# One retention normalisation recorded after a gate projection, and a table load recorded inside a contraction

## The chip, the cores and the metric

The kernel runs on one core of one Trainium2 chip. The metric is the device time of one execution in microseconds (us), as the median of several runs. Its engines are named as in the profile: PE (TensorE, matrix products), PEld (its weight loads), DVE (VectorE), ACT (ScalarE), POOL (GpSimd) and SP (SyncE, which issues the transfers). Each has one queue and takes its instructions in the order of that queue, and waits on semaphores where it needs another engine's result.

## The reference

The computation is one hybrid decoder layer on 256 tokens of width 1024, in float32: a SwiGLU block, a mixer, and a second SwiGLU block, each behind an RMS normalisation that a condition vector modulates. Cut to the mixer and to the branch that the change touches:

```python
def retention_branch(q, k, v, g, positions, norm_w):
    ...
    scores = jnp.einsum('bclhd,bcshd->bchls', qc, kc) * decay_mask
    y_intra = jnp.einsum('bchls,bcshe->bclhe', scores, vc)
    ...
    y = (y_intra + y_inter).reshape(bsz, s, h_, dv).astype(v.dtype)
    y = rms_normalize(y).reshape(bsz, s, RET_V_DIM) * norm_w
    return y * jax.nn.silu(g)

def hybrid_mixer(u, ...):
    proj = u @ w_in
    z, xbc, dt_raw, q, k, v, g, gate_ssd_raw, gate_ret_raw = jnp.split(proj, splits, axis=-1)
    y_ssd = ssd_branch(...) @ w_br_ssd
    y_ret = retention_branch(...) @ w_br_ret
    gate_ssd = jax.nn.sigmoid(gate_ssd_raw + gate_b_ssd)
    gate_ret = jax.nn.sigmoid(gate_ret_raw + gate_b_ret)
    return (gate_ssd * y_ssd + gate_ret * y_ret) @ w_out
```

There are 8 retention heads. Each has a score product, a value product of 256 columns, its own RMS normalisation, and a gate silu(g).

## The kernel before, in words

**Products.** Nearly every product with a weight runs as three PE passes: both operands are split into a rounded high part and a low rest, and `mm3` (L143 to L151) adds high·high, low·high and high·low. A weight block of 128x2048 numbers comes by one transfer on SP's queue into one of four staging buffers (`wst`). `half` (L130) then makes two operands of it: ACT rounds 1024 columns (L135, a CAST into `wh`) and DVE subtracts (L136). There are four `wh` buffers, so two weight blocks are in hand at a time. `pair_project` (L293) uses one block: 24 PE passes for each of two `wh` buffers, 48 in all. `split_into` (L139) does the same to an activation tile of 128x512: L140 on ACT, L141 on DVE.

**PSUM.** Two pools of four buffers each: `proj` for the weight products, `misc` for everything else. A `misc` buffer is handed to a new tile only when the last reader of the old one is done.

**The retention steps.** Three steps work on a head `n`, and one on a pair of heads:

- `rs.n` (`ret_scores`): two PE products (L876, L877) into a `misc` buffer, and two DVE products with the decay mask (L879, L880). The DVE rows are the last readers of that buffer.
- `rv.n` (`ret_values`): four PE products (L888, L889 twice) into a `misc` buffer `py`, a square on ACT (L891), a sum on DVE (L892), and the split of that sum (`sqh` on ACT L767, `sql` on DVE L768).
- `rn.n` (`ret_norm`): `rstd` multiplies that split by a matrix of ones (two PE products, L219, into another `misc` buffer), then ACT does Ln and Exp (L181, `rs`), DVE refines the root in four instructions (L224, L225, L226, L227; L225 is the last reader of the mean's buffer), two DVE instructions multiply `py` by it and the norm weight (L902, the last readers of `py`), one multiplies by the gate (L905), and `split_into` makes the operands (L140, L141) that the branch product reads.
- `br.p.q` (`branch`): the product of head pair `p` with one half `q` of `w_br_ret`, 48 passes. It needs `rn` of both heads of the pair.

`g.h.p` (`silu_half`) is one gate projection and a Silu on ACT (L181). `ada` is one piece of the condition product: one transfer, and two DVE instructions over 128x1024 (L193).

**Tables.** Ln and Exp lie in one function table of ACT, Silu in another, Sigmoid in a third. `need` (L572) notes which table is loaded and records a load (L173) when the next step wants another; `table` ties a load behind every lookup of the table before it.

**What sets the order.** `ORDER` (L52) is a string of step names; the steps are recorded in that order. A scheduler then lays out each engine's queue: a step that was recorded earlier goes first, but an instruction whose operands it takes to be late is passed by others. So the queues differ from `ORDER` in detail, and one step moved can reorder the queues for some 200 instructions around it.

**The end of the mixer.** After `ORDER` the two branches are combined, the table for Ln and Exp is loaded (L939), and `contract` (L328) multiplies by `mix_w_out` in four blocks. After each output tile the residual's closing function adds it and squares it; after each block `each` is called, which here records a piece of `ada`. Then `modulated` (L259) normalises, with the Ln and Exp in `rstd`.

## Time and profile before

| What | Value |
|---|---|
| median of 3 runs | 835.44 us (835.42 to 836.02) |
| the profiled execution: own time, span of its instructions | 836.0 us, 833.9 us |
| granted PE clock, mean | 0.998 |
| busy: PE, PEld, DVE, ACT, POOL | 820.4, 795.0, 664.1, 517.2, 10.3 us |
| table loads on ACT | 30, each 1.283 us |
| DMA | 193.13 MB, 232 GB/s on average |

The span runs from the first to the last instruction; the execution's own time is 2.1 us longer. A PE row of the timeline is shown with its modelled end, and rows overlap since the products are pipelined: what counts is the distance from one start to the next. "Idle" in a row is time in which an engine had nothing running, and the name behind it is what ended that.

### The profile page before, as it was taken

The numbers are of one execution on the slowest core, as the hardware profiler recorded it, in microseconds if no ns is written. First come the engines' busy times: TensorE is split into PE (matmuls) and PEld (weight loads), VectorE is DVE, ScalarE is ACT, GpSimd is POOL, SyncE is SP. The second block draws the span as 40 slices with busy tenths as digits, with TensorE's granted clock in tenths as the row PEclk, the third lists the DMA queues.
The fourth block names the chain that finished last, engine by engine and source line by source line (L and its number), as shares of the span: only waits on it lengthen the run. The fifth ranks groups of instructions, "written<-read, shape, count | busy, mean of one in ns | idle before, by whom it ended". The sixth has DMA issues, their size and how long they took to land. (4 is left out here: it accounts for less than half of the span.)

```text
span 833.9 us, 16144 instructions
## 1 busy us (share of the span) xinstructions
PE 820.4 (98%) x6734; PEld 795.0 (95%) x6734; DVE 664.1 (80%) x1002; ACT 517.2 (62%) x743; POOL 10.3 (1%) x21
## 2 busy tenths in 40 slices
PE   7999999999999999999999999999999999999996
PEld 6999999999999989999999999999999999999896
DVE  5999899977989987787898768977979985455463
ACT  6665454555898787766565569665558655545342
POOL 0000000000200010000000000000000000000000
PEclk9999999999999999999999999999999999999999
DMA  9998889854695564536657754645555685455521
GB/s 365 415 398 328 303 330 389 343 193 153 231 312 185 183 215 180 197 132 240 233 181 293 253 202 152 223 182 197 207 202 194 263 326 204 152 203 177 189 90 50
DMA packets 30586, 193.13 MB, mean 232 GB/s; under 512 B 3489, under 2 KB 4129, under 8 KB 10034
## 3 DMA queue, kind: packets, MB, share of 16 engines
q1 hardware_dynamic: 28656, 186.40, 60.4%
q0 software_dynamic: 1568, 5.28, 2.0%
q8 instruction: 52, 0.85, 0.4%
q10 hardware_dynamic: 290, 0.44, 0.2%
q14 instruction: 20, 0.16, 0.1%
HBM read 191.02 MB, written 1.08 MB: 230 GB/s over the span
## 5 line engine op out<-in xcount | busy, mean ns | idle before, releaser
L136 DVE TENSOR_TENSOR wh<-wst,wh 128x1024 fp32r<-128x1024 f32 (+1 forms) x263 | 317.2, 1210 | 109.1 <-ACT wh L135 108.4
L135 ACT CAST wh<-wst 128x1024 fp32r<-128x1024 f32 (+1 forms) x263 | 272.7, 1039 | 169.1 <-PE proj L151 129.8
L149 PE MATMUL proj<-uh,wh 128*128 128x256 f32 (+1 forms) x1160 | 322.3, 278 | 0.0
L150 PE MATMUL proj<-ul,wh 128*128 128x256 f32 (+1 forms) x1160 | 321.8, 277 | 0.1
L151 PE MATMUL proj<-uh,wh 128*128 128x256 f32 (+1 forms) x1160 | 321.3, 277 | 0.0
L150 PEld LDWEIGHTS proj<-ul,wh 128*128 128x128 f32 x1160 | 217.8, 188 | 1.1 <-DVE ul L428 0.3
L151 PEld LDWEIGHTS proj<-uh,wh 128*128 128x128 f32 x1160 | 217.8, 188 | 0.5 <-DVE wh L406 0.2
L149 PEld LDWEIGHTS proj<-uh,wh 128*128 128x128 f32 x1160 | 217.8, 188 | 0.3 <-ACT wh L135 0.2
L149 PE MATMUL proj<-s,wh 128*128 128x256 f32 x312 | 86.9, 280 | 0.3 <-ACT s L140 0.3
L150 PE MATMUL proj<-s,wh 128*128 128x256 f32 x312 | 86.3, 278 | 0.0
L151 PE MATMUL proj<-s,wh 128*128 128x256 f32 x312 | 86.2, 277 | 0.0
L149 PEld LDWEIGHTS proj<-s,wh 128*128 128x128 f32 x312 | 58.4, 188 | 0.7 <-ACT s L140 0.5
L150 PEld LDWEIGHTS proj<-s,wh 128*128 128x128 f32 x312 | 58.5, 188 | 0.3 <-issue 0.2
L151 PEld LDWEIGHTS proj<-s,wh 128*128 128x128 f32 x312 | 58.6, 188 | 0.0
L193 DVE SCALAR_TENSOR_TENSOR ada<-ada,cb 128x1024 f32<-128x1024 f32 x48 | 57.5, 1219 | 0.0
L145 PE MATMUL proj<-uh,wh 128*128 128x256 f32 x152 | 42.0, 276 | 0.0
L146 PE MATMUL proj<-uh,wh 128*128 128x256 f32 x152 | 42.0, 276 | 0.0
L147 PE MATMUL proj<-ul,wh 128*128 128x256 f32 x152 | 42.0, 276 | 0.0
L149 PE MATMUL proj<-ah,wh 128*128 128x256 f32 x152 | 42.0, 276 | 0.0
L150 PE MATMUL proj<-al,wh 128*128 128x256 f32 x152 | 42.0, 276 | 0.0
L151 PE MATMUL proj<-ah,wh 128*128 128x256 f32 x152 | 42.0, 276 | 0.0
L181 ACT ACTIVATE s<-proj 128x512 f32<-128x512 f32 x33 | 19.7, 597 | 33.0 <-PE proj L151 32.9
(271 smaller groups left out, 1399.6 us busy)
## 6 DMA issues: line engine op xcount, KB each, us to landing
wst<-in_mix_w_in_dram SPq DMA_DIRECT2D x52, 1024.0 KB, 4.9
wst<-in_ffn_w_in_dram SPq DMA_DIRECT2D x43, 1024.0 KB, 5.8
wst<-in_ffn_w_out_dram SPq DMA_DIRECT2D x17, 1024.0 KB, 5.2
ada<-in_ada_w_dram SPq DMA_DIRECT2D x16, 1024.0 KB, 9.0
wst<-in_ada_w_dram SPq DMA_DIRECT2D x12, 1024.0 KB, 4.9
ada<-in_ada_w_dram SPq DMA_DIRECT2D x16, 512.0 KB, 12.6
wst<-in_w_br_ssd_dram SPq DMA_DIRECT2D x8, 1024.0 KB, 5.7
wst<-in_w_br_ret_dram SPq DMA_DIRECT2D x8, 1024.0 KB, 4.9
```

Source lines behind the costliest of these rows:

```text
L135: act.copy(hi, v)
L136: dve.tensor_tensor(lo, v, hi.bitcast(F32), ALU.subtract)
L145: pe.matmul(o, l[1], r[0], start=False, stop=False, skip_group_check=skip)
L146: pe.matmul(o, l[0], r[0], start=False, stop=False, skip_group_check=skip)
L147: pe.matmul(o, l[0], r[1], start=False, stop=False, skip_group_check=skip)
L149: pe.matmul(o, l[0], r[0], start=first, stop=False, skip_group_check=skip)
L150: pe.matmul(o, l[0], r[1], start=False, stop=False, skip_group_check=skip)
L151: pe.matmul(o, l[1], r[0], start=False, stop=last, skip_group_check=skip)
L181: phase["uses"].append(act.activation(*args, **kw).ins)
L193: dve.scalar_tensor_tensor(st[:, i, :], st[:, i, :], 1.0, cb, ALU.mult, ALU.mult, accum_out=raw[:, j, f0 + i:f0 + i + 1])
```

## The change

Two edits. In `ORDER`, `rn.0 g.1.0` becomes `g.1.0 rn.0`: the normalisation of the first head is recorded after the first gate projection of the second pair. And the load of the table for Ln and Exp is recorded by the function that `contract` calls after each block, the first time it is called, and no longer ahead of `contract`.

```diff
-    "rv.0 rs.1 rv.1 rn.0 g.1.0 ada rs.2 rn.1 rs.3 rv.2 g.1.1 rv.3 br.0.0 rn.2 rn.3 br.0.1 rs.4 g.2.0 "
+    "rv.0 rs.1 rv.1 g.1.0 rn.0 ada rs.2 rn.1 rs.3 rv.2 g.1.1 rv.3 br.0.0 rn.2 rn.3 br.0.1 rs.4 g.2.0 "
...
         while ada_todo[0][0] == 7:
             ada_next()
-        table("natural_log_exp_and_others")
+        later = ["natural_log_exp_and_others"]
+
+        def each():
+            if later:
+                table(later.pop())
+            ada_next(6)
         am = scale_col(V_N3, 7)
...
         contract("mix_w_out", 8, lambda kt: at(mh[kt // 4], al, kt % 4),
-                 residual(5, 1.0, am, ha, u, 6), lambda: ada_next(6))
+                 residual(5, 1.0, am, ha, u, 6), each)
```

What this does to the queues is shown at three places.

**First place: ACT, right after the Silu of the last projection of the first pair, `g.0.1` (`proj_5800`).** `wh_6018` and `wh_6045` before, `wh_6016` and `wh_6043` now, are the weights of `g.1.1`; `misc_5856` and `misc_5874` are the values of heads 0 and 1; `misc_5887` is the mean of head 0; `proj_5889` is the projection `g.1.0`.

```order
 L181 ACTIVATE s_5733<-proj_5800 128x512
-L173 ACT_TABLE_LOAD
+L135 CAST wh_6016<-wst_6013 128x1024
 L891 ACTIVATE rsq_5861<-misc_5856 128x512
-L135 CAST wh_6018<-wst_6015 128x1024
+L135 CAST wh_6043<-wst_6013 128x1024
 L767 ACTIVATE sqh_5864<-rsq_5861 128x256
-L135 CAST wh_6045<-wst_6015 128x1024
 L891 ACTIVATE rsq_5879<-misc_5874 128x512
-L181 ACTIVATE rs_5890<-misc_5887,epsc 128x256
-L181 ACTIVATE rs_5890<-rs_5890 128x256
-L173 ACT_TABLE_LOAD
```

A load and its return are gone here, the weights of `g.1.1` are rounded earlier, and the Ln and Exp of head 0 stand behind the Silu of `g.1.0`. The program has 28 table loads instead of 30. On DVE the subtraction for `wh_6016` and the sum of head 0 (L892) stand ahead of the mask rows L879 and L880 of head 1 (`m_5871`), which were first before:

```order
+L136 TENSOR_TENSOR wh_5917<-wst_5887,wh_5917 128x1024
+L136 TENSOR_TENSOR wh_6016<-wst_6013,wh_6016 128x1024
+L892 TENSOR_TENSOR rsq_5861<-rsq_5861 128x256
 L879 TENSOR_TENSOR m_5871<-misc_5868,xe_5724 128x256
 L880 TENSOR_TENSOR m_5871<-misc_5868,xe_5724 128x128
-L892 TENSOR_TENSOR rsq_5861<-rsq_5861 128x256
```

**Second place: PE between the projection `g.1.1` and the first branch product.** Before, the mean of head 1 (`misc_5979`) and the scores of heads 2 and 3 (`misc_5972`, `misc_5996`) stand ahead of the 48 passes of `g.1.1` (`proj_6017`):

```order
L876 MATMUL misc_5972<-s_4902,s_4970 128x256
L877 MATMUL misc_5972<-s_4902,s_4970 128x128
L219 MATMUL misc_5979<-sqh_5882,onesr 128x256 [waits DVE_49,Activation_49]
L219 MATMUL misc_5979<-sql_5883,onesr 128x256 [waits DVE_49]
L876 MATMUL misc_5996<-s_4902,s_4970 128x256 [waits DVE_49,PE_49]
L877 MATMUL misc_5996<-s_4902,s_4970 128x128
L149 MATMUL proj_6017<-uh_146,wh_6018 128x256
```

Now the mean of head 0 and the scores of head 2 stand ahead of `g.1.1`, and behind its 48 passes follow the mean of head 1 (`misc_5977`), the scores of head 3 (`misc_5994`), the values of head 2 (`misc_6000`) and the first passes of the branch product, whose operand `s_5961`, `s_5962` is the split of heads 0 and 1:

```order
L219 MATMUL misc_5977<-sqh_5882,onesr 128x256 [waits DVE_49,Activation_49]
L219 MATMUL misc_5977<-sql_5883,onesr 128x256
L876 MATMUL misc_5994<-s_4902,s_4970 128x256 [waits DVE_49,PE_49]
L877 MATMUL misc_5994<-s_4902,s_4970 128x128
L888 MATMUL misc_6000<-m_5974,s_3668 128x256 [waits DVE_49]
L889 MATMUL misc_6000<-m_5974,s_3668 128x128
L149 MATMUL proj_6090<-s_5961,wh_6087 128x256 [waits Activation_49]
L149 MATMUL proj_6119<-s_5961,wh_6116 128x256
L149 MATMUL proj_6187<-s_5961,wh_6184 128x256 [waits PE_49]
L149 MATMUL proj_6216<-s_5961,wh_6213 128x256 [waits PE_49,Activation_49]
L150 MATMUL proj_6090<-s_5962,wh_6087 128x256 [waits DVE_49]
```

(L888 and L889 come twice here; the second two are left out.) By the semaphore values, the first of these waits for DVE's L225 of head 0, which frees the mean's buffer, and L876 waits for the second L902 of head 0, which frees `py` of head 0. The first four passes of the branch product go to four different `proj` tiles.

**Third place: DVE, the root of head 1 and what follows it.** Before:

```order
L224 TENSOR_TENSOR rt_5983<-rs_5982 128x256
L225 SCALAR_TENSOR_TENSOR rt_5983<-misc_5979,rt_5983 128x256
L226 TENSOR_SCALAR rt_5983<-rt_5983 128x256
L227 TENSOR_TENSOR rs_5982<-rs_5982,rt_5983 128x256
L768 SCALAR_TENSOR_TENSOR sql_6011<-rsq_6007,sqh_6010 128x256
L902 SCALAR_TENSOR_TENSOR m_5990<-misc_5874,col,rs_5982 128x256 x2
L879 TENSOR_TENSOR m_5999<-misc_5996,st_5970 128x256
```

Now a weight subtraction, the split of head 0 (L141), the sum of head 2 (L892) and both instructions of an `ada` piece (L193) stand between the steps of that root, and L879, L905 and L880 behind them:

```order
L224 TENSOR_TENSOR rt_5981<-rs_5980 128x256
L136 TENSOR_TENSOR wh_6213<-wst_6182,wh_6213 128x1024
L141 TENSOR_TENSOR s_5962<-m_5957,s_5961 128x512
L225 SCALAR_TENSOR_TENSOR rt_5981<-misc_5977,rt_5981 128x256
L193 SCALAR_TENSOR_TENSOR wst_6386,raw<-wst_6386,cb 128x1024
L226 TENSOR_SCALAR rt_5981<-rt_5981 128x256
L892 TENSOR_TENSOR rsq_6005<-rsq_6005 128x256
L227 TENSOR_TENSOR rs_5980<-rs_5980,rt_5981 128x256
L193 SCALAR_TENSOR_TENSOR wst_6386,raw<-wst_6386,cb 128x1024
L902 SCALAR_TENSOR_TENSOR m_5988<-misc_5874,col,rs_5980 128x256 x2
L879 TENSOR_TENSOR m_5997<-misc_5994,st_5969 128x256
```

From the gate projections of the third pair (`g.2.0`, `g.2.1`) on, all queues are again in the order of before, up to the end. That includes the second edit: in ACT's queue the table load for the last normalisation stands where it stood, between the last Sigmoid of the gate (L181) and the CAST of the second half of the first `mix_w_out` block.

## The prediction

> **What bounds the kernel now.** I read the page's busy shares first, then the busy time by stretch around the moved steps and around the last normalisation of the mixer, then PE's own waits, then the timeline of each engine.

> ```profile
> PE 820.4 (98%) x6734; PEld 795.0 (95%) x6734; DVE 664.1 (80%) x1002; ACT 517.2 (62%) x743; POOL 10.3 (1%) x21
> ...
> 480.00:495.00 15.00, 15.00 (x132) 14.95 (x132) 10.99 (x15) 7.80 (x11) 0.00 (x0) 1.00 0.76 267
> 495.00:510.00 15.00, 14.52 (x112) 13.77 (x112) 11.40 (x19) 14.22 (x18) 0.00 (x0) 1.00 0.42 154
> 620.00:640.00 20.00, 19.70 (x172) 19.51 (x171) 18.22 (x32) 15.90 (x31) 0.00 (x0) 1.00 0.45 158
> ...
> PE misc L219 <- ACT sqh L767: 0.5, 1, 0.5
> PE misc L219 <- ACT sq L248: 0.8, 1, 0.8
> ```

> The columns of a stretch are its length, the busy time of PE, PEld, DVE, ACT and POOL, PE's clock, the DMA share and GB/s. PE is never idle from 480 to 495 us and issues 132 passes there, so a pass takes 15.00/132 = 0.1136 us. From 495 to 510 ACT is the one that is full, 14.22 of 15 us, and PE loses 0.48 us to `sqh`. So time is lost or won only where PE waits; whatever else moves is free. PE's order and its waits at the first place:

> ```profile
> 498.57 0.59 PE L888 MATMUL misc<-m,s 128*128 128x256 f32 x2
> 499.88 0.60 PE L876 MATMUL misc<-s,s 128*128 128x256 f32 x2
> 500.45 0.36 PE L149 MATMUL proj<-uh,wh 128*128 128x256 f32 x1
> 501.00 0.28 PE L150 MATMUL proj<-ul,wh 128*128 128x256 f32 x1
> 501.26 0.70 PE L888 MATMUL misc<-m,s 128*128 128x256 f32 x2
> 502.45 0.38 PE L889 MATMUL misc<-m,s 128*128 128x128 f32 x2
> 503.32 0.39 PE L219 MATMUL misc<-sqh,onesr 128*128 128x256 f32 x1 [0.48 <-ACT sqh L767]
> ...
> 511.00 0.28 PE L150 MATMUL proj<-ul,wh 128*128 128x256 f32 x1
> 511.26 0.70 PE L888 MATMUL misc<-m,s 128*128 128x256 f32 x2
> ```

> A head's values take 499.88 - 498.57 = 1.31 us on PE, a head's scores 500.45 - 499.88 = 0.57 us. PE is late three times: L888 at 501.26 where 501.11 was free (0.15), L219 at 503.32 where 501.26 + 1.31 = 502.57 was free (0.75), L888 at 511.26 where 511.11 was free (0.15). That is 1.05 us, and it is all that the first edit can win here.

> **Prices.** ACT and DVE from their timeline and from the groups between 495 and 530 us (count, then busy time and mean ns of one):

> ```profile
> 499.52 0.59 ACT L181 ACTIVATE s<-proj 128x512 f32<-128x512 f32 x1
> 500.13 1.28 ACT L173 ACT_TABLE_LOAD   x1
> 501.42 0.60 ACT L891 ACTIVATE rsq<-misc 128x512 f32<-128x512 f32 x1
> 501.92 1.04 ACT L135 CAST wh<-wst 128x1024 fp32r<-128x1024 f32 x1
> ...
> 617.77 1.28 ACT L173 ACT_TABLE_LOAD   x1
> ...
> L135 ACT CAST wh<-wst 128x1024 fp32r<-128x1024 f32 x10 | 10.4, 1044 | 0.2 <-PE proj L151 0.2
> L173 ACT ACT_TABLE_LOAD x8 | 10.3, 1283 | 0.1
> L181 ACT ACTIVATE rs<-misc,epsc 128x256 f32<-128x256 f32 x4 | 1.9, 474 | 0.3 <-PE misc L219 0.3
> L767 ACT ACTIVATE sqh<-rsq 128x256 fp32r<-128x256 f32 x4 | 1.7, 418 | 0.2 <-DVE rsq L892 0.2
> L181 ACT ACTIVATE rs<-rs 128x256 f32<-128x256 f32 x4 | 1.7, 418 | 0.0
> L140 ACT CAST s<-m 128x512 fp32r<-128x512 f32 x2 | 1.2, 620 | 0.8 <-DVE m L905 0.8
> ```

> ```profile
> 499.64 1.23 DVE L136 TENSOR_TENSOR wh<-wst,wh 128x1024 fp32r<-128x1024 f32 x1 [0.95 <-ACT wh L135]
> 500.79 0.42 DVE L879 TENSOR_TENSOR m<-misc,xe 128x256 f32<-128x256 f32 x1
> ...
> L902 DVE SCALAR_TENSOR_TENSOR m<-misc,col,rs 128x256 f32<-128x256 f32 x6 | 2.6, 477 | 0.0
> L193 DVE SCALAR_TENSOR_TENSOR wst<-wst,cb 128x1024 f32<-128x1024 f32 x2 | 2.4, 1220 | 0.0
> L905 DVE TENSOR_TENSOR m<-m,s 128x512 f32<-128x512 f32 x3 | 2.1, 685 | 0.0
> L892 DVE TENSOR_TENSOR rsq<-rsq 128x256 f32<-128x256 f32 x4 | 1.7, 424 | 1.8 <-ACT rsq L891 1.8
> L225 DVE SCALAR_TENSOR_TENSOR rt<-misc,rt 128x256 f32<-128x256 f32 x4 | 1.7, 422 | 0.1
> L224 DVE TENSOR_TENSOR rt<-rs 128x256 f32<-128x256 f32 x4 | 1.7, 422 | 0.0
> L141 DVE TENSOR_TENSOR s<-m,s 128x512 fp32r<-128x512 f32 x2 | 1.4, 688 | 0.4 <-ACT s L140 0.4
> L227 DVE TENSOR_TENSOR rs<-rs,rt 128x256 f32<-128x256 f32 x3 | 1.3, 424 | 0.1
> L226 DVE TENSOR_SCALAR rt<-rt 128x256 f32<-128x256 f32 x3 | 0.9, 293 | 0.1
> L879 DVE TENSOR_TENSOR m<-misc,st 128x256 f32<-128x256 f32 x2 | 0.8, 416 | 0.0
> L880 DVE TENSOR_TENSOR m<-misc,st 128x128 f32<-128x128 f32 x2 | 0.6, 282 | 0.0
> ```

> An instruction that waits for nothing starts 0.1 us before the last one ends (501.42 + 0.60 against 501.92); a table load starts behind its end. From one engine to another I count 0.05 us (L879 ends at 501.21, L888 starts at 501.26).

> **Part one, what it removes.** Two table loads, 2 x 1.283 us of ACT, and the wait of 0.75 us for `sqh`. The trace shows nothing beside the load itself: 0.1 us of idle time ahead of eight of them, and the next instruction 0.01 us behind. [...]

> **What it moves, walked through in the new order.** All times are those of the old trace up to the Silu at 499.52, and reckoned from there.

> First, the mask of head 1. The CAST of `wh_6016` now follows the Silu directly, 500.02 to 501.06; DVE subtracts 501.11 to 502.33, sums head 0 from 502.25, and comes to L879 at 502.60, which ends at 503.0 where it ended at 501.21. PE has 15 passes ahead of the values of head 1, not five, and is there at 501.11 + 10 x 0.1136 = 502.25. It waits to 503.05: 0.8 us. So the first two old waits, 0.9 us together, come back as one of about their size.

> Second, the bank waits. PE goes on: values 1.31, 33 passes 3.75, two passes for the mean of head 0 (0.23), scores of head 2 (0.57), 48 passes of `g.1.1` (5.45), and stands at 514.35 before the mean of head 1. Meanwhile head 0 is normalised: `g.1.0` ends at 508.3, then Silu, `sqh` of head 1 and the table load run to 510.55, Ln to 511.0, a CAST to 512.0, Exp to 512.3. DVE does a weight subtraction (512.05 to 513.27), L224, and another subtraction whose CAST waits until PE has freed its buffer (513.5 to 514.75); then L225 ends at 515.1, L227 at 515.85, the second L902 at 516.8, L879 at 517.1, L905 at 517.7, L880 at 517.9. PE's next three steps wait for three of these: the mean of head 1 for L225 (515.15, 0.8 us), after 0.23 the scores of head 3 for L902 (516.85, 1.45), after 0.57 the values of head 2 for L880 (517.95, 0.55). In the old order 48 passes of `g.1.1` lay between the mean of head 1 and the branch product; now they are spent before.

> Third, the branch product. The values end at 519.25; the split's high part is ready (Ln and Exp of head 1 to 516.5, load to 517.85, CAST to 518.45), four passes take PE to 519.7, and L141 stands behind a weight subtraction, 519.3 to 520.0: 0.35. Twenty more passes end at 522.3. Now PE needs the mask L879 of head 3 for the next values, and DVE has ahead of it L225, L193, L226, L892, L227, L193 and twice L902: from 519.95 at 0.08 us less than their rows each, with 0.05 where one needs the last one, that is 524.25 for its start and 524.7 for its end: 2.45. L889 then waits for L880, behind L905, to 525.55: 0.25. Then the rest of these values, 0.9 us (1.31 less the first L888), and two passes, to 526.7, and the low part of head 1's split (CAST from 525.35, L141 to 526.7), with which PE goes on at 526.75: 0.05.

> The sum is 0.8 + 0.8 + 1.45 + 0.55 + 0.35 + 2.45 + 0.25 + 0.05 = 6.7 us of waits, for 1.05 us before: 5.65. One wait more is likely and not walked through, the low part of head 3's sum (L768), which now stands behind a weight subtraction: between nothing and 0.3 us, taken as 0.15. That makes 5.8 us. From `g.2.0` on the queues are as before, and PE is full again, so nothing gives it back.

> **Part two costs and gains nothing.** The load at 617.77 stands between the same neighbours in ACT's queue. PE's wait of 0.8 us for the last square (L248) and the normalisation behind it stay.

> **Bounds.** An ada piece is in this chain: its transfer is issued when the subtraction that ends at 513.27 frees its staging buffer. If it were 1 us late, the third wait would grow by that; if each of six more changes between float32 products and passes costs what L149 at 500.45 has over its neighbours (0.36 for 0.28 us), 0.5 us more. The other way, each of the eight waits ends a chain of five to ten instructions, and 0.3 us of error in each is 2.4 us: 3.4 to 7.3 us in all.

> Against the profiled execution: span 833.9 + 5.8 = 839.7 us, own time 836.0 + 5.8 = 841.8 us. That execution is 0.6 us above the median of the runs shown, so the median is expected at 835.44 + 5.8 = 841.2 us; its own range is 838.8 to 842.7.

> **Rivals.**

> (a) Nothing net. DVE is far enough ahead that L225, L902 and L880 are done when PE comes, and the old waits only change place: 835.4 us. For it: DVE was 80% busy, and ACT gains 2.6 us of room. Against: L225 sits behind a subtraction whose CAST needs the first half of `g.1.1` done, which no earlier start of ACT can mend.

> (b) Faster. Both parts do what they are named for: the three waits go (1.05 us), and the wait at the last normalisation (0.8 us), because the load is out of its way: 833.6 us. For it: ACT was full for 15 us at the first place. Against: the load at 617.77 keeps its neighbours, and the three waits are replaced by the eight above.

> (c) A slower clock. PE waits seven times within 12 us. If the clock halves for some time after that, the 24 passes of the branch product's half that follow cost twice 0.1136 us, 2.7 us more: 843.9 us. The point from which it decides is a wait that holds PE long enough; the trace has granted clock 1.00 in every stretch quoted, with waits up to 0.8 us. [...]

> **How the numbers follow.** Forecast 0.85, (a) 0.06, (b) 0.05, (c) 0.04. What a measurement of this kernel can tell from no change is about 0.2%, 1.7 us. (a) lies within, (b) just outside, the forecast and (c) outside on the slow side: faster 0.05, same 0.06, slower 0.89. The range is widened a little past the forecast's own on both sides, towards a half-hidden second group (the three bank waits gone: 838.4) and (c): 838.2 to 843.8.

> **What would show it.** PE's waits by releaser: L219 and L876 on DVE (L225, L902) near 515 and 517, L888 on DVE near 518 and near 525, L150 on L141 near 520; 28 table loads; the stretch 510 to 527 with PE idle 5 to 6 us; the tail's rows shifted by 5.8 us and else as before. It is wrong if PE is full from 505 to 525, or if the shift at `g.2.0` is not the shift at the end.

## The result, and the profile after

| | median | all executions | against before |
|---|---|---|---|
| before | 835.80 us | 835.42 to 836.02 (6) | |
| the change | 841.24 us | 840.70 to 842.54 (6) | 1.0068, 95% interval 1.0059 to 1.0078 |

The change costs 5.4 us; 841.2 was forecast. In its profiled execution the own time is 840.76 us and the span 838.9, against 836.0 and 833.9. (Of all executions in the sections below one, of 2134.2 us in the run with the ada piece moved and filler, was disturbed and is left out.)

Busy time of the whole kernel, and its PE waits (line waited for: us in total, times, longest):

```profile
PE 822.7 (98%) x6734; PEld 796.8 (95%) x6734; DVE 663.8 (79%) x1002; ACT 514.3 (61%) x741; POOL 10.3 (1%) x21
...
PE misc L888 <- DVE m L879: 1.3, 2, 0.7
PE misc L876 <- DVE m L902: 1.2, 1, 1.2
...
PE misc L219 <- DVE rt L225: 0.5, 1, 0.5
```

The wait for `sqh` (L767) is gone, and ACT is 2.9 us less busy. Three waits on DVE take its place: on masks (L879), on L902 and on L225. The busy time by stretch, in the columns of the prediction's first fence:

```profile
495.00:510.00 15.00, 14.41 (x116) 13.90 (x115) 9.27 (x12) 11.07 (x15) 0.00 (x0) 1.00 0.40 151
510.00:525.00 15.00, 12.40 (x83) 11.36 (x81) 12.89 (x26) 9.79 (x14) 0.00 (x0) 0.89 0.44 144
525.00:540.00 15.00, 14.86 (x122) 14.27 (x121) 10.61 (x21) 10.66 (x16) 0.00 (x0) 1.00 0.37 137
```

From 495 to 510 us ACT went from 14.22 us busy to 11.07, and PE gained nothing from it. From 510 to 525 PE issues 83 passes where it issued 124. It stood idle for 2.60 us, and the clock, 1.00 before, is 0.89. That second figure was not in the forecast. PE's timeline there:

```profile
515.19 0.35 PE L219 MATMUL misc<-sqh,onesr 128*128 128x256 f32 x1 [0.50 <-DVE rt L225]
...
516.89 0.67 PE L876 MATMUL misc<-s,s 128*128 128x256 f32 x2 [1.23 <-DVE m L902]
...
520.01 1.20 PE L149 MATMUL proj<-s,wh 128*128 128x256 f32 x4
521.01 0.41 PE L150 MATMUL proj<-s,wh 128*128 128x256 f32 x1
521.23 0.41 PE L151 MATMUL proj<-s,wh 128*128 128x256 f32 x1
...
522.11 0.28 PE L151 MATMUL proj<-s,wh 128*128 128x256 f32 x1
522.23 0.28 PE L149 MATMUL proj<-s,wh 128*128 128x256 f32 x1
...
523.60 0.28 PE L151 MATMUL proj<-s,wh 128*128 128x256 f32 x1
524.61 0.70 PE L888 MATMUL misc<-m,s 128*128 128x256 f32 x2 [0.73 <-DVE m L879]
```

The bank waits stand where they were forecast (515.15 and 516.85). But the branch product's passes at 521 start 0.22 us apart, those at 522 again 0.12. So PE reaches the values of head 3 at 523.7 and not at 522.3, and waits 0.73 us for a mask that I expected it to await for 2.45. In half-microsecond stretches the clock begins to fall inside 518.00 to 518.50 (mean 0.97, so 0.03 us at half) and is back inside 521.50 to 522.00 (mean 0.62, so 0.38 us at half): half clock from 518.47 to 521.88, 3.41 us.

So there are two questions for the runs. Do the waits come from where the walk had them? And what does the half clock cost, which I had as a rival with a chance of 0.04?

### The profile page after: what moved, and what is told of

Same layout as the page of the kernel before. It is cut to its first block, busy times and chain, and to the rows that moved or that the text cites. A ratio compares the mean times of both kernels' runs of the same rounds, so it can differ in the third digit from the quotient of the medians.

```text
span 838.9 us, 16141 instructions
## 1 busy us (share of the span) xinstructions
PE 822.7 (98%) x6734; PEld 796.8 (95%) x6734; DVE 663.8 (79%) x1002; ACT 514.3 (61%) x741; POOL 10.3 (1%) x21
## 5 line engine op out<-in xcount | busy, mean ns | idle before, releaser
L136 DVE TENSOR_TENSOR wh<-wst,wh 128x1024 fp32r<-128x1024 f32 (+1 forms) x263 | 317.0, 1209 | 115.2 <-ACT wh L135 114.6
L135 ACT CAST wh<-wst 128x1024 fp32r<-128x1024 f32 (+1 forms) x263 | 272.5, 1039 | 168.8 <-PE proj L151 130.1
L149 PE MATMUL proj<-uh,wh 128*128 128x256 f32 (+1 forms) x1160 | 322.6, 278 | 0.0
L151 PE MATMUL proj<-uh,wh 128*128 128x256 f32 (+1 forms) x1160 | 321.3, 277 | 0.0
L150 PE MATMUL proj<-ul,wh 128*128 128x256 f32 (+1 forms) x1160 | 321.3, 277 | 0.0
L150 PEld LDWEIGHTS proj<-ul,wh 128*128 128x128 f32 x1160 | 218.0, 188 | 0.6 <-issue 0.2
L149 PEld LDWEIGHTS proj<-uh,wh 128*128 128x128 f32 x1160 | 218.1, 188 | 0.3 <-ACT wh L135 0.2
L151 PEld LDWEIGHTS proj<-uh,wh 128*128 128x128 f32 x1160 | 217.9, 188 | 0.5 <-DVE wh L406 0.2
L149 PE MATMUL proj<-s,wh 128*128 128x256 f32 x312 | 87.2, 282 | 0.3 <-ACT s L140 0.3
L150 PE MATMUL proj<-s,wh 128*128 128x256 f32 x312 | 86.4, 278 | 0.0
L151 PE MATMUL proj<-s,wh 128*128 128x256 f32 x312 | 86.2, 277 | 0.0
L149 PEld LDWEIGHTS proj<-s,wh 128*128 128x128 f32 x312 | 58.8, 190 | 0.7 <-ACT s L140 0.5
L150 PEld LDWEIGHTS proj<-s,wh 128*128 128x128 f32 x312 | 58.9, 189 | 0.3 <-issue 0.2
L151 PEld LDWEIGHTS proj<-s,wh 128*128 128x128 f32 x312 | 58.8, 189 | 0.0
L193 DVE SCALAR_TENSOR_TENSOR ada<-ada,cb 128x1024 f32<-128x1024 f32 x48 | 57.5, 1218 | 0.0
L149 PE MATMUL proj<-ah,wh 128*128 128x256 f32 x152 | 42.0, 276 | 0.0
L150 PE MATMUL proj<-al,wh 128*128 128x256 f32 x152 | 42.0, 276 | 0.0
L151 PE MATMUL proj<-ah,wh 128*128 128x256 f32 x152 | 42.0, 276 | 0.0
L181 ACT ACTIVATE s<-proj 128x512 f32<-128x512 f32 x33 | 19.7, 597 | 34.3 <-PE proj L151 34.3
## 6 DMA issues: line engine op xcount, KB each, us to landing
ada<-in_ada_w_dram SPq DMA_DIRECT2D x16, 512.0 KB, 12.8
```

Source lines behind the costliest of these rows:

```text
L135: act.copy(hi, v)
L136: dve.tensor_tensor(lo, v, hi.bitcast(F32), ALU.subtract)
L149: pe.matmul(o, l[0], r[0], start=first, stop=False, skip_group_check=skip)
L150: pe.matmul(o, l[0], r[1], start=False, stop=False, skip_group_check=skip)
L151: pe.matmul(o, l[1], r[0], start=False, stop=last, skip_group_check=skip)
L181: phase["uses"].append(act.activation(*args, **kw).ins)
```

## Experiments

Theory: the first edit alone makes the loss, by letting a head's mean and scores queue behind `misc` buffers that are freed late, and by the DVE chain behind them. The rivals were a share of the second edit, the half clock as part of the price, and a chain that is late whatever buffers there are. The first four kernels, the next three and the last two were each compared with runs of the kernel before that they share (835.69, 835.71 and 835.74 us).

### Each edit alone

The first edit alone:

```diff
-    "rv.0 rs.1 rv.1 rn.0 g.1.0 ada rs.2 rn.1 rs.3 rv.2 g.1.1 rv.3 br.0.0 rn.2 rn.3 br.0.1 rs.4 g.2.0 "
+    "rv.0 rs.1 rv.1 g.1.0 rn.0 ada rs.2 rn.1 rs.3 rv.2 g.1.1 rv.3 br.0.0 rn.2 rn.3 br.0.1 rs.4 g.2.0 "
```

> This kernel has the first edit alone: the gate projection ahead of head 0's normalisation in the written order; the table load stands ahead of the output contraction as before. Theory (all of the loss comes from the first edit, through PE's waits): 841.2 us, 5.4 us above the kernel before, with the same waits of PE between 510 and 525 us as in the changed kernel, 28 table loads and an end of the profile like the changed kernel's. Rival (the second edit has a share, for good or ill): a time more than 0.8 us away from 841.2 us.

Measured: median 842.49 us (840.69, 842.36, 842.62, 843.41), ratio 1.0078, interval 1.0064 to 1.0092. The whole loss is there. The median is 1.3 us above the changed kernel's, which by the letter of the expectation speaks for the rival. But the fastest executions agree, 840.69 and 840.70, and both kernels have executions near 840.7 and near 842.5. Its profiled execution is one of the longer ones (842.62), and shows why:

```profile
502.13 0.28 PE L147 MATMUL proj<-ul,wh 128*128 128x256 f32 x1
502.99 0.70 PE L888 MATMUL misc<-m,s 128*128 128x256 f32 x2 [0.59 <-DVE m L879]
...
514.44 0.28 PE L151 MATMUL proj<-uh,wh 128*128 128x256 f32 x1
515.22 0.36 PE L219 MATMUL misc<-sqh,onesr 128*128 128x256 f32 x1 [0.50 <-DVE rt L225]
515.41 0.28 PE L219 MATMUL misc<-sql,onesr 128*128 128x256 f32 x1
516.91 0.67 PE L876 MATMUL misc<-s,s 128*128 128x256 f32 x2 [1.23 <-DVE m L902]
...
517.95 0.70 PE L888 MATMUL misc<-m,s 128*128 128x256 f32 x2
...
519.28 0.72 PE L149 MATMUL proj<-s,wh 128*128 128x256 f32 x4
520.02 0.38 PE L150 MATMUL proj<-s,wh 128*128 128x256 f32 x1
...
522.36 0.28 PE L151 MATMUL proj<-s,wh 128*128 128x256 f32 x1
524.63 0.70 PE L888 MATMUL misc<-m,s 128*128 128x256 f32 x2 [2.00 <-DVE m L879]
524.98 0.46 PE L219 MATMUL misc<-sqh,onesr 128*128 128x256 f32 x1
525.43 0.49 PE L889 MATMUL misc<-m,s 128*128 128x128 f32 x2
```

The branch product runs at full clock here (520.02 to 522.36), the wait for the mask is 2.00 us long, and L888 starts at 524.63, as in the changed kernel's 524.61. The half clock comes 7.7 us later, from 526.14 to 529.55, on passes that nothing hides: 3.41 us at half clock are 1.7 us of work lost, and this execution is 1.86 us longer than the changed kernel's profiled one. So the time is about 840.7 us when the half clock falls ahead of a wait, and about 842.5 when it falls behind it. That this also tells the changed kernel's own executions apart is inferred: of them only that of 840.76 us has a trace. The 843.41 us is more than this accounts for.

The second edit alone:

```diff
-        table("natural_log_exp_and_others")
+        later = ["natural_log_exp_and_others"]
+
+        def each():
+            if later:
+                table(later.pop())
+            ada_next(6)
...
-                 residual(5, 1.0, am, ha, u, 6), lambda: ada_next(6))
+                 residual(5, 1.0, am, ha, u, 6), each)
```

> This kernel has the second edit alone: the order of before, and the table load written behind the first part of the output contraction. Theory: the load keeps its neighbours in ACT's queue, PE's wait of 0.8 us for the last square (L248) stays, and the time is that of the kernel before within 0.3 us, 835.7 us. Rival: the load leaves the path of the last normalisation and PE's wait of 0.8 us goes, 834.9 us.

Measured: 835.62 us, ratio 0.9999, interval 0.9991 to 1.0008: nothing. ACT's timeline of this kernel:

```profile
616.46 0.84 ACT L181 ACTIVATE s<-proj,col 128x256 f32<-128x256 f32 x2 [1.62 <-PE proj L151]
617.32 1.28 ACT L173 ACT_TABLE_LOAD   x1
618.61 1.05 ACT L135 CAST wh<-wst 128x1024 fp32r<-128x1024 f32 x1
...
622.52 1.05 ACT L135 CAST wh<-wst 128x1024 fp32r<-128x1024 f32 x1 [2.34 <-issue]
```

The load has its old neighbours. Nor does ACT run short of time behind it: ACT is idle for 2.34 us before the second CAST behind the load, and PE's wait for the last square is 0.8 us as before.

### The DVE chain ahead of head 3's mask

Of head 3's wait I had said that two L193 of an ada piece stand in the chain. This takes them out:

```diff
-    "rs.5 g.2.1 rv.4 ada rv.5 br.1.0 rn.4 rn.5 g.3.0 ada rs.6 br.1.1 rs.7 g.3.1 rv.6 rv.7 br.2.0 "
+    "rs.5 g.2.1 rv.4 rv.5 br.1.0 rn.4 rn.5 g.3.0 ada ada rs.6 br.1.1 rs.7 g.3.1 rv.6 rv.7 br.2.0 "
```

> The changed kernel with one piece of the adaptive vectors' work (ada), two L193 of 1.22 us on DVE, moved later by seven steps, out of the queue ahead of head 1's second L902 and the mask L879 of head 3. Theory A (PE's clock halves for 3.4 us between 518.3 and 521.9, and the half clock lies hidden behind the DVE chain that ends at 524.6): without the two L193 that chain ends 2.4 us earlier, but PE reaches the values of head 3 only at about 523.7 us, so the wait of 0.73 us at L888 goes and little else: 0.7 to 1.1 us less than the changed kernel, 840.1 to 840.5 us, with the granted clock below 0.95 in 510 to 525 us. Theory B (the waits alone count, as my walk had it at full clock): 2.1 us less, 839.1 us.

Measured: median 839.58 us (838.59, 839.13, 839.58, 839.74, 840.82), ratio 1.0048, interval 1.0035 to 1.0062. The median lies between the two theories. The profiled execution is the fastest; there the clock was 1.00 from 510 us to behind the last product, and DVE's timeline reads

```profile
520.26 0.29 DVE L226 TENSOR_SCALAR rt<-rt 128x256 f32<-128x256 f32 x1
520.59 0.43 DVE L227 TENSOR_TENSOR rs<-rs,rt 128x256 f32<-128x256 f32 x1
520.95 0.42 DVE L892 TENSOR_TENSOR rsq<-rsq 128x256 f32<-128x256 f32 x1
521.29 0.87 DVE L902 SCALAR_TENSOR_TENSOR m<-misc,col,rs 128x256 f32<-128x256 f32 x2
522.08 0.41 DVE L879 TENSOR_TENSOR m<-misc,st 128x256 f32<-128x256 f32 x1
```

The mask is done at 522.49, 2.06 us sooner than in the changed kernel (524.14 + 0.41), and the execution is 2.1 us under that kernel's fastest: what the walk says at full clock. An execution with a half clock near 518 to 522 would lose about 1.2 us of it, since PE would come to the values of head 3 at 523.7 and not at 522.54; three of the five lie 0.5 to 1.2 us above the fastest. That those are half clock is inferred, since they have no trace. The 840.82 is more than this accounts for.

### Keeping PE busy through its waits

If idle PE causes the half clock, filler should remove it. Twenty passes of 128x256 are put ahead of the branch product's first pass, into the PSUM tile that this pass then starts anew; their result is overwritten and no other engine does more:

```diff
+                if (n, g, q, f2) == ("r", 0, 0, 0):
+                    for _ in range(20):
+                        pe.matmul(ps[:, 0, :], u[0][:, 0, :P], u[0][:, 0, :], start=True, stop=True,
+                                  skip_group_check=True)
```

> The changed kernel with 20 more passes (the 128x256 form, 0.1136 us each, their result overwritten) ahead of the branch product's first pass, standing where PE is idle between 514.5 and 519.3 us. Theory A (PE's clock halves because PE is mostly idle there, and that costs nothing since the DVE chain ends later): granted clock 1.00 in 510 to 525 us, passes of the branch product 0.11 us apart, the wait of L888 on the mask L879 of head 3 back from 0.73 to about 2.4 us, and the time unchanged, 841.2 us within 0.4. Theory B (the half clock is part of the price): 1.5 to 2 us less, 839.3 to 839.7 us. Theory C (the clock halves for another reason than idle time): granted clock still below 0.95, and 841.2 us.

Measured: median 841.97 us (840.72, 841.18, 841.97, 842.07, 842.11), ratio 1.0070, interval 1.0057 to 1.0083. Of theory A two points came: the clock is 1.00 from 510 to 525, and PE's wait for the mask is 1.95 us again. The median is 0.7 us above the 841.2, outside the 0.4, but the executions lie within the changed kernel's own range (840.70 to 842.54), so no change of time is shown. In the profiled execution (842.11) the half clock appeared later, at 525.19 to 528.60, behind that longer wait, as in the run of the first edit alone. In this profile's stretches of 3.41 us:

```profile
514.95:518.36 3.41, 3.27 (x25) 3.22 (x26) 3.31 (x9) 3.35 (x5) 0.00 (x0) 1.00 0.63 264
...
521.78:525.19 3.41, 1.46 (x10) 1.07 (x9) 3.41 (x10) 0.52 (x2) 0.00 (x0) 1.00 0.72 243
525.19:528.60 3.41, 3.41 (x15) 3.11 (x14) 1.52 (x4) 1.20 (x3) 0.00 (x0) 0.50 0.66 271
```

With filler the first gap holds 3.27 us of PE work and no half clock follows it. The unfilled stretch with 1.46 us of work is followed by one of exactly half clock. Theory B falls (no gain of 1.5 to 2 us), and so does C.

The same filler with the ada piece moved:

> Both edits at once: the ada piece moved later and the 20 filling passes. Theory A (half clock hidden in the changed kernel, exposed once the DVE chain is shorter): the filler keeps the clock at 1.00, PE reaches the values of head 3 near 522.3 us, and the whole 2.1 us come: 839.1 us, 1.0 to 1.4 us less than with the ada piece moved alone. Theory B (clock irrelevant): the same time as with the ada piece moved alone.

Measured: median 838.6 us (838.59, 838.60, 838.62, 838.77), ratio 1.0034, interval 1.0021 to 1.0048. That is 1.0 us below the ada piece moved alone, and the spread of 2.2 us is now 0.2. Theory A holds, with the time a little under its 839.1; the 2.1 us against the changed kernel's fastest execution is the walk's.

Then both gaps are filled, with 18 more passes ahead of the second half of the branch product (the edit is shown against the run with filler):

```diff
-                if (n, g, q, f2) == ("r", 0, 0, 0):
-                    for _ in range(20):
+                fill = {("r", 0, 0, 0): 20, ("r", 0, 1, 0): 18}.get((n, g, q, f2), 0)
+                if fill:
+                    for _ in range(fill):
```

> The changed kernel with 38 filling passes: 20 where PE is idle between 514.5 and 519.3 us, as in the run with filler above, and 18 ahead of the second half of the branch product, where PE waits for the mask L879 of head 3 (2.0 us with the first filler). Theory A (the changed kernel's executions differ by up to 1.8 us because the half clock, when a stretch of 3.4 us before was busy less than about 60%, falls on work that is not hidden): with both gaps filled the clock stays at 1.00 everywhere between 500 and 540 us, and every execution takes 840.7 us within 0.3. Theory B (the spread has another cause): executions between 840.7 and 842.5 us as without filler.

Measured: 840.82 us, five executions from 840.76 to 840.84, ratio 1.0061, interval 1.0048 to 1.0075. The row from 500 to 540 us:

```profile
500.00:540.00 40.00, 38.87 (x312) 37.55 (x311) 29.88 (x56) 26.47 (x38) 0.00 (x0) 1.00 0.45 158
```

PE does 38 passes of no use, 4.3 us of work, and the kernel takes what the changed kernel's fastest executions take, to 0.1 us: the passes fit into time that waits had taken. The spread of 1.8 us is down to 0.08. So the changed kernel's loss is made of about 5.1 us of waits (840.82 less 835.71) and of up to 1.8 us of half clock, by chance of the execution.

### Why head 1's mean came late: `misc` buffers

```diff
-            ps = misc_ps()
+            ps = proj_ps().rearrange("p f t -> p (f t)") if hd in (2, 3) else misc_ps()
             pe.matmul(ps[:, :T], kk[:, :P], q, start=True, stop=True)
```

> The changed kernel, with the scores of heads 2 and 3 written to a PSUM buffer of the projections' pool in place of one of the four of the misc pool, so that they need not wait for a normalisation to free one. Theory A (the waits near 515 to 518 us and much of the one at 524.6 us come of too few misc buffers: scores, values and means queue behind L225 and L902 of the heads before): about 4.1 us of the 5.4 us come back, 836.6 us, PE idle under 2 us between 510 and 525 us, no half clock. Theory B (DVE's and ACT's chain behind the late gate half is the bound, whatever buffer is used): less than 1.5 us comes back, over 839.2 us.

Measured: 836.63 us (836.29 to 838.01, 11 executions), ratio 1.0014, interval 1.0005 to 1.0022: 0.9 us above its kernel before, so 4.5 of the 5.4 us are back. About 4.2 of them are waits (840.82, the time with both gaps filled, less 836.63), the rest, 0.3 us, I take to be half clock, which this profile does not show while PE works. Theory A. PE's timeline of this kernel, and its stretch from 510 to 525:

```profile
508.14 0.60 PE L876 MATMUL proj<-s,s 128*128 128x256 f32 x2
...
509.06 0.45 PE L219 MATMUL misc<-sqh,onesr 128*128 128x256 f32 x1
```

```profile
510.00:525.00 15.00, 14.70 (x118) 14.09 (x117) 12.15 (x27) 11.84 (x18) 0.00 (x0) 1.00 0.24 75
```

The second L219 pair, the mean of head 1, starts at 509.06 instead of 515.19: it is back ahead of the 48 passes of `g.1.1`, and with it the scores of head 3. In the changed kernel four tiles are alive there: the values of heads 0 and 1, the mean of head 0, the scores of head 2. That is all of the `misc` pool, so the mean of head 1 can have a buffer only when L225 of head 0 has read its own. ACT shows what follows: the Ln of both heads (x2) now run together at 510.32, where the changed kernel has them at 510.57 and 515.70.

```profile
509.03 1.28 ACT L173 ACT_TABLE_LOAD   x1
510.32 0.84 ACT L181 ACTIVATE rs<-misc,epsc 128x256 f32<-128x256 f32 x2
```

The run does not separate the buffer from the new queue order that it allows, since both come together. What stays of the loss, 0.9 us, has a wait of 0.60 us for the mask of head 1 in it, behind the CAST of `wh_6016`, as forecast.

### The other way round

The runs say that normalising later costs. So the step is moved earlier, with the wider choice of buffers:

```diff
-    "ada k.0 bs.3.0 bs.3.1 k.2 ada ada q.2 q.1 gs.3 gs.2 q.3 k.1 gs.1 k.3 ada rs.0 g.0.0 gss g.0.1 "
-    "rv.0 rs.1 rv.1 rn.0 g.1.0 ada rs.2 rn.1 rs.3 rv.2 g.1.1 rv.3 br.0.0 rn.2 rn.3 br.0.1 rs.4 g.2.0 "
...
+    "ada k.0 bs.3.0 bs.3.1 k.2 ada ada q.2 q.1 gs.3 gs.2 q.3 k.1 gs.1 k.3 ada rs.0 gss rv.0 rs.1 "
+    "g.0.0 ada rn.0 g.0.1 rv.1 g.1.0 rs.2 rs.3 rn.1 rv.2 rv.3 g.1.1 br.0.0 rn.2 rs.4 br.0.1 rn.3 "
...
-            ps = misc_ps()
+            ps = proj_ps().rearrange("p f t -> p (f t)") if hd in (2, 3) else misc_ps()
```

> The opposite of the first edit: the normalisation of head 0 is recorded ahead of the last gate projection of the first pair, its values and the scores of head 1 earlier still, and the scores of heads 2 and 3 go to a buffer of the projections' pool as in the run that moved them. The load of the table stands as before. Theory (each step reaches PE's queue only when its operands are done): of the three old waits of 1.05 us in all between 498 and 512 us, some 0.3 us is left, so 0.8 us less than the kernel before, 834.9 us, about as much as the interval of this comparison can tell. Rival: what the steps gain there, ACT's other table loads and the weights' rounding give back: within 0.3 us of the kernel before, or over it.

Measured: 834.59 us (11 executions) against 835.74, ratio 0.9987, interval 0.9979 to 0.9996. The stretches of this kernel:

```profile
480.00:495.00 15.00, 14.90 (x124) 14.49 (x123) 12.81 (x20) 9.35 (x12) 0.00 (x0) 1.00 0.77 281
495.00:510.00 15.00, 15.00 (x125) 14.73 (x125) 10.26 (x19) 11.80 (x16) 0.00 (x0) 1.00 0.40 141
510.00:525.00 15.00, 15.00 (x125) 14.70 (x125) 11.98 (x20) 12.15 (x18) 0.00 (x0) 1.00 0.43 151
```

PE is busy throughout from 495 to 525 us; 0.10 us is lost before. And with order alone (in both edits the steps behind those shown keep their order and only move to other lines):

```diff
-    "ada k.0 bs.3.0 bs.3.1 k.2 ada ada q.2 q.1 gs.3 gs.2 q.3 k.1 gs.1 k.3 ada rs.0 g.0.0 gss g.0.1 "
-    "rv.0 rs.1 rv.1 rn.0 g.1.0 ada rs.2 rn.1 rs.3 rv.2 g.1.1 rv.3 br.0.0 rn.2 rn.3 br.0.1 rs.4 g.2.0 "
...
+    "ada k.0 bs.3.0 bs.3.1 k.2 ada ada q.2 q.1 gs.3 gs.2 q.3 k.1 gs.1 k.3 ada rs.0 gss g.0.0 rv.0 "
+    "rs.1 g.0.1 rv.1 ada rn.0 g.1.0 rs.2 rn.1 rs.3 rv.2 rv.3 g.1.1 br.0.0 rn.2 br.0.1 rs.4 rn.3 "
...
```

> Order alone, no other buffer: the values of head 0 and the scores of head 1 are recorded ahead of the last gate projection of the first pair, the normalisation of head 0 directly behind the values of head 1 and ahead of the gate projection of the second pair, as before. Theory: the three old waits of 1.05 us are replaced by one of about 0.6 us near 510 us: 0.5 us less than the kernel before, 835.2 us, which is under what the comparison can tell. Rival: no gain or a loss, over 835.6 us.

Measured: 834.88 us (11 executions), ratio 0.9988, interval 0.9979 to 0.9997. Its PE has one wait left there, 0.49 us at 510.00 for L902, where about 0.6 was expected. Both are faster than the kernel before, by 1.15 and 0.86 us where 0.8 and 0.5 were expected, with intervals that end just under 1; the two are not told apart. The gain is small because only 1.05 us of waiting was there to be won.

## Why the prediction was right, point by point

The time was right (841.2 forecast, 841.24 measured), the cause was right, and one rival with a small chance took part in it. The walk's waits, against those in the trace of the first edit alone, where PE runs at full clock until 526.14 us; each is the start of the waiting row less the time at which the passes ahead of it would have let PE on, reckoned with the prediction's own durations (the 0.19 in the last row is the distance of the two L219 at 515.22 and 515.41):

| Wait | forecast | measured | from the rows |
|---|---|---|---|
| values of head 1 on mask L879 | 0.8 | 0.75 | 502.99 - (502.13 + 0.11) |
| mean of head 1 on L225 | 0.8 | 0.67 | 515.22 - (514.44 + 0.11) |
| scores of head 3 on L902 | 1.45 | 1.46 | 516.91 - (515.22 + 0.23) |
| values of head 2 on L880 | 0.55 | 0.47 | 517.95 - (516.91 + 0.57) |
| L150 of the branch product on L141 | 0.35 | 0.29 | 520.02 - (519.28 + 4 x 0.1136) |
| values of head 3 on mask L879 | 2.45 | 2.16 | 524.63 - (522.36 + 0.11) |
| its second part on L880 | 0.25 | 0.26 | 525.43 - (524.98 + 0.19) |
| sum | 6.65 | 6.06 | |

- **The first edit's removal.** Two loads fewer, 28 in all, and the wait for `sqh` gone: as forecast. That ACT's room would help nobody was right too.
- **The sum.** Seven waits are together 0.6 us smaller than forecast, half of that in head 3's. The 20 passes ahead of it take 522.47 - 520.02 = 2.45 us instead of 2.27, which shortens that wait by 0.18; the mask itself ends where the DVE chain was forecast to end, at about 524.6 instead of 524.7. The two small terms, 0.05 and 0.15, can't be read off. The net of waits is then 6.06 + 0.18 - 1.05 = 5.2 us against 5.8. Without half clock the kernel takes 840.8 us (both gaps filled), 5.1 us above before: the walk was 0.7 us too large.
- **The half clock**, my rival (c), chance 0.04. It did come, for 3.41 us. What failed is the step that says when, "a wait that holds PE long enough". In the changed kernel it came with no wait above 1.5 us (the longest 1.23), after a stretch in which PE was busy 1.91 of 3.41 us, while in the run with both gaps filled the clock stayed at 1.00 with PE idle for 1.47 us. The price of 2.7 us was also off, 1.7 us for 3.41 us at half clock, and nothing where it falls ahead of the wait for head 3's mask.
- **That the median met the forecast to 0.1 us** is therefore part luck: waits 0.7 us smaller than forecast, and a half clock that adds between nothing and 1.8 us to an execution.
- **Rival (a)**, nothing net, fell by the rows at 515 and 517 us. L225 runs at 514.62 on DVE, behind two weight subtractions (512.01 and 513.49), as the walk had it. The CAST for the second, at 512.19, follows the Exp on ACT with no idle time between, so the trace does not show it held up by the first half of `g.1.1`, the reason that I gave. The run with other buffers shows that the lateness of L225 and L902 costs PE little once two score tiles need not wait for the buffers that they free. **Rival (b)**, faster: the three old waits of 1.05 us did go, but seven of 6.06 us came in their place; they can be had, but by normalising earlier.
- **Part two at nothing**: right, shown by the second edit alone.
- **The tail.** The table load stands at 622.75 us in the changed kernel's profile (617.77 before), 5.0 us later where 5.8 was forecast, and nothing is given back: the spans differ by 5.0 too.
- **A sign that did not come.** From 510 to 527 us PE was to be idle for 5 to 6 us. It is idle for 2.60 us in the changed kernel and for 3.88 with the first edit alone. Part of this is the measure: the profile shows a pass 0.28 us long that lets the next one start after 0.11, so each wait looks some 0.17 us shorter than it is.

Open: why executions of the kernel before differ by about 1 us among themselves (835.30 to 836.35 in the last series), the single 840.82 of the ada piece moved and 843.41 of the first edit alone, the spread of the run with other buffers (836.29 to 838.01), and whether a share of busy time decides on the half clock.

## What to carry to other kernels

Before a step is moved behind another, count the tiles that stay alive across the new gap: here all four buffers of a pool were taken, and a mean, then the scores, then the values and the product behind them stood behind 48 passes, until two score tiles were given buffers elsewhere. The room that an engine got (ACT, 2.9 us) was worth nothing here, since another chain set the end, and the step that starts a long chain cost 5 us when it was moved later and gained about 1 us when it was moved earlier. Where a kernel's executions fall into groups, look at the granted clock in short stretches: the spread can be one event that falls before a wait in one execution and behind it in the next.

## What the runs showed of the hardware

```profile
515.06:518.47 3.41, 1.91 (x9) 1.47 (x10) 3.33 (x9) 3.35 (x6) 0.00 (x0) 1.00 0.64 264
518.47:521.88 3.41, 3.41 (x16) 3.23 (x15) 3.41 (x8) 2.46 (x4) 0.00 (x0) 0.50 0.40 111
521.88:525.29 3.41, 2.68 (x20) 2.29 (x19) 3.41 (x10) 0.52 (x2) 0.00 (x0) 1.00 0.71 235
```

```profile
515.90:519.31 3.41, 2.25 (x13) 1.93 (x13) 3.41 (x8) 3.33 (x6) 0.00 (x0) 1.00 0.46 190
...
522.73:526.14 3.41, 1.51 (x7) 1.17 (x8) 3.26 (x9) 0.62 (x1) 0.00 (x0) 1.00 0.67 226
526.14:529.55 3.41, 3.41 (x17) 3.34 (x17) 0.84 (x2) 1.01 (x2) 0.00 (x0) 0.50 0.42 178
```

Busy times of 1.46 (the run with the first filler), 1.51 and 1.91 in 3.41 us (43, 44 and 56%) were followed by half clock, 2.25 and 2.68 (66 and 79%) were not. The waits near 515 to 518 us are the same in both kernels, but in the one the edges fall so that a stretch holds 1.91 us of work, in the other 2.25. The run with both gaps filled has one more such stretch at its end, cut in the same length back from 836.74 us:

```profile
829.92:833.33 3.41, 1.94 (x17) 1.73 (x15) 2.09 (x6) 2.14 (x6) 0.00 (x0) 1.00 0.03 13
833.33:836.74 3.41, 0.00 (x0) 0.00 (x0) 0.91 (x3) 1.31 (x4) 0.00 (x0) 1.00 0.64 248
```

Here 1.94 us (57%) are followed by full clock, with a longer gap (1.47 us, from the last product's end at 831.86) than the changed kernel's 1.23. So, with the stretch cut there, the longest gap did not decide. Nor do these rows fix a share (the "about 60%" of that run's expectation does not hold for this stretch): 56 and 57% are closer than the measure can carry, since the profile's busy time uses modelled ends, and the 1.91 us are 9 passes with waits between, the 1.94 us 17 passes in a row. A run that would settle it was not made.

In the traces below, the times at which PE's clock changes lie whole multiples of one length apart. In the changed kernel the clock falls again behind the last product, at 835.91 us (the clock of 835.50 to 836.00 is 0.91), 317.44 us after 518.47. With 3.41 us measured for one stretch, that can only be 93 of them, of 317.44/93 = 3.413 us each. In the run with the first filler, 835.80 (the clock of the same half microsecond is 0.80) less 525.19 is 91.0 times that. The changed kernel's trace has such an edge at the start too: the passes at 16.07, 16.29, 16.50 and 16.71 us start 0.21 to 0.22 us apart and those from there on 0.11 to 0.13, and 518.47 less 16.71 is 147.0 times 3.413, although the profile's clock reads 1.00 there. From the changed kernel's 518.47 to the 526.14 of the first edit alone it is 2.25 times. So the edges lie differently against the program in these two executions, and the price of the same waits differs with them.
